# A two-layer decoder on one core: six of eight query tiles by seven block products in place of eight

## The chip, the cores and the metric

The kernel is one program on one core of a Trainium2 chip, written instruction by instruction in a language in which each engine has its own in-order queue and semaphores tie the queues together. The engines are PE (matrix products), DVE (vector), ACT (scalar functions), POOL (general) and SP, which here only starts transfers. POOL starts transfers too. The metric is the time of one execution on the device in microseconds (us).

## The reference

The input is 1024 tokens of width 1024 in float32. Layer 0 mixes tokens with a gated short convolution, layer 1 with sliding-window attention; each is followed by a SwGLU feed-forward network of inner width 2816. What the change touches is the query projection of layer 1:

```python
h = rmsnorm(x, norm_mixer[1])
qkv = h @ w_qkv                      # 1024 x (1024 q + 256 k + 256 v)
q, k = rmsnorm(q, q_gain), rmsnorm(k, k_gain)     # per head of 64
...
scores = einsum('bnqkgd,bnskd->bnkgqs', qb, kw) * scale   # blocks of 128 queries, 256 keys
p = softmax([scores + alibi, masked; sink])[..., :-1]
out = einsum('bnkgqs,bnskd->bnqkgd', p, vw).reshape(1024, 1024) @ w_o
x = x + out
```

There are 16 query heads and 4 key and value heads of 64.

## The kernel before, in words

Activations lie transposed in SBUF, features on partitions and tokens along the free side: `X[k]` is feature block k (128) of the residual stream, 1024 tokens, and `xs[k]` (tags XS0 to XS7) is the normalised operand, kept as a high and a low part in a reduced 32-bit format (`fp32r`). Every large product is a sum of three matmuls of 128x128 weights against 128x512 operands: high by high, high by low, low by high. Weights arrive by SP's transfers in `WR` and are split there into `WH` (high) and `WL` (low) by `Weights.split`, whose cast and subtract go to engines that the caller names.

The convolution, feed-forward and output products already use a scheme of seven block products in place of eight (`SUMS` names which sums of weight blocks it needs; `added_sums` makes these in DRAM by copies on SP and accumulating transfers on POOL). The query projection does not: each of its eight tiles of 128 output features (two heads) is 8 feature blocks times 6 matmuls, 48 in all (`product_step`, lines 161 to 172).

Attention runs so. `project_k` makes the two key tiles `k0` and `k1`, `project_v` two value tiles of 512 tokens. Their results stand in the four PSUM banks of tag "acc" until ACT and DVE have taken them out: `keep_v` scales by the token's factor r, with the high part on ACT and the low on DVE (line 1723); `keep_k` turns the head statistics across partitions with transposes on PE (1746), multiplies the rows by them on DVE (`scale_rows`, 1751), and writes zero-padded high and low halves (1765 to 1767). Query tile 0 follows. Up to here the tile scheduler orders the instructions of each engine. From `keep_q(0, acc)` on, the order is as written: `step` takes one softmax unit (one of 8 query tiles by 8 token blocks) through the letters of

```python
ORDER = "SPTMEDkPHLVOPK"
```

where each P asks the product generator for its next piece, here two matmuls; S is the scores, T and H/L turns, V the product with the values. So a query tile of 24 pieces is 8 steps, and the softmax of unit n runs beside the projection of a later tile, `LAG` steps on.

PSUM has eight banks: four "acc", and P0 to P3. `after_silu` ties instructions to the end of layer 0.

In the layer before, the planner of a `Line` sets the order: `at(t, f)` puts a call at time t of a list by hand, `put` a block product's operands. `half_chain` is a half's token statistics, with `mean`, `guess` and `turn`; `turn` is the transposes that put it across partitions (line 1179 issues them, 1165 makes their input).

## Time and profile before

| | us |
|---|---|
| median of 3 runs | 1933.56 |
| lowest, highest | 1932.24, 1933.91 |
| the profiled execution | 1931.62 |
| its span | 1929.8 |

A profile shows one execution. A row of the timeline has a start, a duration, the engine, the line of the kernel, the operation and its output and input; "x4" means four in a row, and the square bracket names what ended the idle time before. Matmuls overlap, so a matmul's own duration (0.39 us for 128x512) is longer than the distance to the next one's start.

The stretch concerned: layer 0's last product starts at 952.25; the key tiles follow to about 977, the values and the turns to 1005.3, query tile 0 to about 1020, query tiles 1 to 7 to about 1184. Then come the output projection and layer 1's feed-forward network.

### The profile page before, as it was taken

The page shows a single profiled execution, that of the slowest core. Times are in us where ns is not written, and L with a number is a line of the kernel's source. Part 1 is how long each engine was busy: PE and PEld are TensorE (multiplying, and loading weights), DVE is VectorE, ACT ScalarE, POOL GpSimd, SP SyncE. Part 2 cuts the span into 40 slices and gives each one's busy share as a digit, 9 for nine tenths or more (in the row PEclk, how much of TensorE's full clock was granted, in tenths as well). Part 3 has the DMA queues.
Part 4 walks back from the last instruction along what each step waited for, and adds up shares of the span by engine and source line. Part 5 has one row for each costly group of instructions (what it writes and reads, how often), then busy time and mean ns, then how long its engine had stood idle before and what let it go on. Part 6 is the DMA issues. An engine that isn't in the chain of part 4 may idle for free.

```text
span 1929.8 us, 25194 instructions
## 1 busy us (share of the span) xinstructions
PE 1922.1 (100%) x9105; PEld 1608.3 (83%) x9105; DVE 1286.8 (67%) x2223; ACT 877.7 (45%) x1741; POOL 275.7 (14%) x373
## 2 busy tenths in 40 slices
PE   9999999999999999999999999999999999999999
PEld 7888888888888888888898888888888888888887
DVE  8997877975655666555644777788656665665543
ACT  5543464533333334444435887555333333344441
POOL 0011231011101100000014455210111111100000
PEclk9999999999999999999999999999999999999999
DMA  8896695376657638976310000152674576477562
GB/s 314 255 252 144 141 249 156 107 235 191 156 193 210 149 135 298 337 220 206 96 34 23 23 12 18 53 182 76 215 218 135 204 190 166 130 251 267 196 227 102
DMA packets 132077, 326.14 MB, mean 169 GB/s; under 512 B 13680, under 2 KB 25072, under 8 KB 131952
## 3 DMA queue, kind: packets, MB, share of 16 engines
q1 hardware_dynamic: 101520, 228.81, 34.9%
q0 software_dynamic: 30288, 95.70, 20.3%
q8 instruction: 71, 1.16, 0.2%
q14 instruction: 54, 0.44, 0.1%
q10 hardware_dynamic: 144, 0.03, 0.0%
HBM read 261.31 MB, written 130.55 MB: 203 GB/s over the span
## 4 chain that ended last, share of the span: by engine, by line
PE 93%; issue 2%; DVE 2%; DMA 1%; POOL 1%; ACT 1%; SPq 0%; POOLq 0%; ACTq 0%; DVEq 0%
PE acc L996 15%; PE acc L997 15%; PE acc L999 15%; PE P L996 9%; PE P L999 9%; PE P L997 9%; PE acc L167 7%; PE acc L171 3%; PE P L1922 1%; PE P L1746 1%; PE acc L1126 1%; PE P L1947 1%; PE acc L1128 1%; PE acc L1127 1%; PE P L1948 1%
## 5 line engine op out<-in xcount | busy, mean ns | idle before, releaser
L996 PE MATMUL acc<-XS,G 128*128 128x512 f32 x926 | 360.4, 389 | 0.0
L999 PE MATMUL acc<-XS,G 128*128 128x512 f32 x926 | 360.3, 389 | 0.0
L997 PE MATMUL acc<-XS,G 128*128 128x512 f32 x926 | 360.2, 389 | 0.0
L996 PE MATMUL P<-A,G 128*128 128x512 f32 x550 | 214.1, 389 | 0.0
L999 PE MATMUL P<-A,G 128*128 128x512 f32 x550 | 214.0, 389 | 0.0
L997 PE MATMUL P<-A,G 128*128 128x512 f32 x550 | 214.0, 389 | 0.0
L999 PEld LDWEIGHTS acc<-XS,G 128*128 128x128 f32 x926 | 173.9, 188 | 36.1
L996 PEld LDWEIGHTS acc<-XS,G 128*128 128x128 f32 x926 | 173.9, 188 | 36.0
L997 PEld LDWEIGHTS acc<-XS,G 128*128 128x128 f32 x926 | 173.9, 188 | 35.9
L996 PE MATMUL acc<-A,G 128*128 128x512 f32 x442 | 172.1, 389 | 0.0
L999 PE MATMUL acc<-A,G 128*128 128x512 f32 x442 | 172.0, 389 | 0.0
L997 PE MATMUL acc<-A,G 128*128 128x512 f32 x442 | 171.9, 389 | 0.0
L930 DVE TENSOR_TENSOR G<-WR,G 128x512 fp32r<-128x512 f32 (+1 forms) x216 | 144.4, 668 | 29.2 <-ACT G L929 28.4
L930 DVE TENSOR_TENSOR G<-WL,G 128x512 fp32r<-128x512 f32 x168 | 114.9, 685 | 71.1 <-ACT G L929 71.1
L929 ACT CAST G<-WR 128x512 fp32r<-128x512 f32 (+1 forms) x216 | 130.4, 605 | 64.7 <-PE acc L999 27.5
L167 PE MATMUL acc<-XS,WH 128*128 128x512 f32 x480 | 148.2, 408 | 1.1 <-ACT WH L139 0.8
L929 ACT CAST G<-WH 128x512 fp32r<-128x512 f32 (+1 forms) x174 | 104.7, 602 | 86.0 <-PE acc L999 37.8
L930 DVE TENSOR_TENSOR G<-WH,G 128x512 fp32r<-128x512 f32 (+1 forms) x174 | 115.5, 664 | 17.9 <-ACT G L929 17.9
L1327 ACT ACTIVATE G<-G 128x512 f32<-128x512 f32 x88 | 55.8, 634 | 156.8 <-DVE G L1424 151.0
L999 PEld LDWEIGHTS P<-A,G 128*128 128x128 f32 x550 | 103.3, 188 | 21.4
L997 PEld LDWEIGHTS P<-A,G 128*128 128x128 f32 x550 | 103.3, 188 | 21.4
L996 PEld LDWEIGHTS P<-A,G 128*128 128x128 f32 x550 | 103.3, 188 | 21.4
(335 smaller groups left out, 3646.2 us busy)
## 6 DMA issues: line engine op xcount, KB each, us to landing
G<-h SPq DMA_DIRECT2D x70, 512.0 KB, 5.1
s<-in_w_dn SPq DMA_DIRECT2D x32, 704.0 KB, 7.5
h<-X POOLq DMA_DIRECT2D x44, 512.0 KB, 4.6
s<-s POOLq DMA_DIRECT2D x32, 704.0 KB, 7.2
WR<-in_w_gu SPq DMA_DIRECT2D x36, 512.0 KB, 4.6
WH<-in_w_gu SPq DMA_DIRECT2D x36, 512.0 KB, 3.8
h<-X POOLq DMA_DIRECT2D x66, 256.0 KB, 3.3
WR<-s SPq DMA_DIRECT2D x62, 256.0 KB, 3.7
```

Source lines behind the costliest of these rows:

```text
L167: pe.matmul(ps.half(h), wh, xs[:, j, c], start=first and j == 0, stop=False)
L171: pe.matmul(ps.half(h), wl, xs[:, 0, c], start=False, stop=last)
L929: lambda: act.copy(out_hi, raw),
L930: lambda: lo_eng.tensor_tensor(out_lo, raw, plain(out_hi), ALU.subtract),
L996: pe.matmul(ps, w[:, 0, c], x[:, 0, :], start=start and e == 0, stop=False, skip_group_check=True)
L997: pe.matmul(ps, w[:, 0, c], x[:, 1, :], start=False, stop=False, skip_group_check=True)
L999: pe.matmul(ps, w[:, 1, c], x[:, 0, :], start=False, stop=last, skip_group_check=True)
L1126: pe.matmul(ps, hi[:, kc], xs[:, 0, c], start=k == 0, stop=False, skip_group_check=True)
L1127: pe.matmul(ps, hi[:, kc], xs[:, 1, c], start=False, stop=False, skip_group_check=True)
L1128: pe.matmul(ps, lo[:, kc], xs[:, 0, c], start=False, stop=k == n_op - 1, skip_group_check=True)
L1327: state["silu"] = act.activation(x, x, AF.Silu)
L1746: pe.transpose(pb[:, t], wide[:, t], ident)
```

## The change

Query tiles 0 and 1 stay as they were. Tiles 2 to 7 become three pairs; of a pair, the 2x2 blocks (two tiles by the two halves of the tokens, each over even and odd feature blocks) are computed by seven block products of 12 matmuls each, 84 for a pair of tiles in place of 96. `QUERY_ORDER` is the order of the seven. Four of their operands are sums of operand blocks (`operand_sums`: per pair of feature blocks one scale on ACT, four `scalar_tensor_tensor` on DVE, then split in high and low on ACT and DVE); they are stored to `q_ops` in DRAM by POOL, two transfers of 1 MB for each of four calls, and loaded again by SP, 512 KB at a time, for each pair of tiles that uses them (`STREAMED`; 48 loads, in a ring of rooms). The weights come as granules of 256 KB, from a new layout `w_q` of the query weights or from `q_sums`, sums made in layer 0's feed-forward by eight copies and eight accumulating transfers. A granule is split by ACT and POOL.

Other things move. Both key weights are loaded ahead of the value weights. The four `operand_sums` stand between the calls that make keys and values, the last ahead of the second key tile's statistics. `step`'s pieces are two, one, two and two matmuls in turn in the pairs (24 pieces for 42 matmuls). `LAG` is 12. `keep_q` of a paired tile finds its values in SBUF, where DVE and ACT have added the blocks (`finish`), and takes its squares from there. SP is now in the hand-written order too. The output weights' early tiles are split at other steps and under other tags, and the feed-forward of layer 1 names other slots. In layer 0 the second half's `half_chain` and the first `scale` and `put` calls come 1.6 and 1.2 later.

The program has these counts, before and after: PE 128x512 matmuls 7785 and 7749; DVE 16 more `scalar_tensor_tensor` of 128x512, 28 more `tensor_tensor` of 128x512; ACT 18 more casts of 128x256, 16 more casts and 10 more activations of 128x512, 6 fewer copies; POOL 18 more subtracts of 128x256 and 16 more transfers; SP 71 more transfers.

The core of the diff:

```diff
-LAG = 10
+LAG = 12
+QUERY_ORDER = (0, 5, 2, 6, 1, 3, 4)
+STREAMED = (5, 2, 3, 4)
...
-            at(t + 3.9, mean)
-            at(t + 3.95, guess)
-            at(t + 5.7, turn)
+            d = 1.6 if whole and h else 0.0
+            at(t + 3.9 + d, mean)
+            at(t + 3.95 + d, guess)
+            at(t + 5.7 + d, turn)
...
-                at(t + 6.8 + 2.6 * p, scale, 1, 2 * p + 1)
-                put(6, p, lambda p=p: X[2 * p + 1][:, hi_half], t + 7.6 + 2.6 * p, minus=True)
+                at(t + 8.0 + 2.6 * p, scale, 1, 2 * p + 1)
+                put(6, p, lambda p=p: X[2 * p + 1][:, hi_half], t + 8.8 + 2.6 * p, minus=True)
...
+        def operand_sums(p, tags):
+            tiles = [slot(tag, (P, 2, 2, HALF), F32R) for tag in tags]
+            t1, t2, t3, t4 = (a[:, i] for a in tiles for i in (0, 1))
...
+            act.activation(b12, X[even][:, hi_half], AF.Copy, scale=ge)
+            dve.scalar_tensor_tensor(raw(t1), X[even][:, lo_half], ge, b12, ALU.mult, ALU.subtract)
+            dve.scalar_tensor_tensor(raw(t2), X[odd][:, hi_half], mo, raw(t1), ALU.mult, ALU.subtract)
+            dve.scalar_tensor_tensor(raw(t3), X[odd][:, hi_half], go, b12, ALU.mult, ALU.subtract)
+            dve.scalar_tensor_tensor(raw(t4), X[odd][:, lo_half], mo, raw(t2), ALU.mult, ALU.subtract)
+            for t in (t1, t2, t3, t4):
+                act.copy(t[:, 0], raw(t))
+                dve.tensor_tensor(t[:, 1], raw(t), plain(t[:, 0]), ALU.subtract)
+            for i, a in enumerate(tiles):
+                nc.gpsimd.dma_start(
+                    q_ops[p, 2 * i : 2 * i + 2].rearrange("k p c -> p k c"), plain(a).rearrange("p k j c -> p k (j c)")
+                )
...
+        for g in range(2):
+            w_k.append(Weights())
+            w_k[g].load(w_qk[NK + g], 0, NK)
         k0 = project_k(0)
+        operand_sums(0, ("A2", "A3"))
...
+        operand_sums(1, ("A0", "A1"))
         r = token_r()
...
+        operand_sums(2, ("A4", "A5"))
+        v += [slot(f"A{4 + q}", (P, 4, NKV, 2, HD), F32R) for q in range(2)]
         v_ps = project_v(0)
         keep_v(0, v_ps)
         keep_k(0, k0[0], y0)
+        operand_sums(3, ("A2", "A3"))
         st = bank("acc")
         head_stats(st, k1[1], 0, NB)
...
+            def split_granule(j, i):
+                g, c = grans[j % 2], slice(i * 2 * P, (i + 1) * 2 * P)
+                act.copy(g[:, 0, c], raws[:, j % 2, c])
+                pool.tensor_tensor(g[:, 1, c], raws[:, j % 2, c], plain(g[:, 0, c]), ALU.subtract)
...
+                for j, (u, k) in enumerate(seq):
+                    plan(0, lambda j=j: split_granule(j + 1, 0))
+                    plan(0.5, lambda j=j: split_granule(j + 1, 1))
+                    load_granule(j + 2)
...
+                    for p in range(NK // 2):
+                        x = operand(k, p)
...
+                        for i, (w, b) in enumerate(((0, 0), (0, 1), (1, 0))):
+                            pe.matmul(
+                                ps, g[:, w, c], x[:, b, :], start=begin and i == 0, stop=end and i == 2, skip_group_check=True
+                            )
+                            n += 1
...
+                            if last and k in STREAMED:
+                                after_use(used["n"])
+                                used["n"] += 1
+                            if last and end:
+                                finish(u, k)
+                            if n % 7 in (2, 4, 5, 0):
+                                yield
...
-        with tc.manual_schedule(engines={E.PE, E.Activation, E.DVE, E.Pool}):
+        with tc.manual_schedule(engines={E.PE, E.Activation, E.DVE, E.Pool, E.SP}):
             keep_q(0, acc)
             w = load_w(w_qk[1], NK, dve, pool)
+            pairs = query_pairs()
...
+            keep_q(1, acc, pairs.odd_raw)
+            work = pairs.work()
+            for _ in range(NB * (NK - 2)):
...
+                step(work)
+            run(work)
```

In the program the engines' queues change at these places. First DVE, at the end of the values and the second key tile. Names: `A_1123` and `A_1163` are value tiles, `acc` the banks that hold the projected values, `G_1151` (before) and `G_1154` (after) the second key tile, `G_1131` the first. Before:

```order
L1723 SCALAR_TENSOR_TENSOR A_1123_7690<-acc_8033,r_7774,A_1123_7690 128x4x64
L1723 SCALAR_TENSOR_TENSOR A_1123_7690<-acc_8082,r_7774,A_1123_7690 128x4x64
L1751 TENSOR_TENSOR G_1151_7860<-G_1151_7860,P_1171_8141 128x512
L1723 SCALAR_TENSOR_TENSOR A_1123_7690<-acc_8082,r_7774,A_1123_7690 128x4x64
L1751 TENSOR_TENSOR G_1151_7860<-G_1151_7860,P_1172_8148 128x512
L1765 CAST A_1173_8154<-G_1151_7860 64x1024 x2
L1766 TENSOR_TENSOR A_1174_8155<-G_1151_7860,A_1173_8154 64x1024
L1767 TENSOR_TENSOR A_1174_8155<-G_1151_7860,A_1173_8154 64x1024
L1766 TENSOR_TENSOR A_1174_8155<-G_1151_7860,A_1173_8154 64x1024
L1767 TENSOR_TENSOR A_1174_8155<-G_1151_7860,A_1173_8154 64x1024
```

The value subtracts (L1723) stand among the row scalings of the second key tile (L1751), ahead of its split (L1765 to L1767). The changed program, from just behind the two row scalings of the second key tile (L1786):

```order
L1724 SCALAR_TENSOR_TENSOR A_1171_8086<-X_885_6220,cst_61,A_1172_8087 128x512
L1726 SCALAR_TENSOR_TENSOR A_1172_8087<-X_890_6243,cst_61,A_1172_8087 128x512
L1725 SCALAR_TENSOR_TENSOR A_1171_8086<-X_890_6243,minus_gain_7707,A_1171_8086 128x512
L1730 TENSOR_TENSOR A_1172_8087<-A_1172_8087 128x512
L1800 CAST A_1169_8076<-G_1131_7776 64x1024 x2
L1727 SCALAR_TENSOR_TENSOR A_1172_8087<-X_890_6243,minus_gain_7707,A_1171_8086 128x512
L1730 TENSOR_TENSOR A_1171_8086<-A_1171_8086 128x512 x2
L1801 TENSOR_TENSOR A_1170_8077<-G_1131_7776,A_1169_8076 64x1024
L1802 TENSOR_TENSOR A_1170_8077<-G_1131_7776,A_1169_8076 64x1024
L1801 TENSOR_TENSOR A_1170_8077<-G_1131_7776,A_1169_8076 64x1024
L1802 TENSOR_TENSOR A_1170_8077<-G_1131_7776,A_1169_8076 64x1024
L1757 SCALAR_TENSOR_TENSOR A_1162_7953<-acc_7955,r_7828,A_1162_7953 128x4x64
```

Three sums of the last `operand_sums` call (L1724 to L1726), a fourth (L1727), its subtracts (L1730) and the first key tile's split (L1800 to L1802) now stand between the row scaling and the first value subtract (L1757); seven more value subtracts follow, with the last L1730 after the second of them, and then the second key tile's split.

On POOL, at the same place, before:

```order
L1775 MEMSET G_1124_7691 128x64
L142 ISA
L142 TENSOR_TENSOR WL_8167<-WR_8164,WH_8166 128x1024
L893 DMA s_1_113<-s_1_113 256x512
L142 TENSOR_TENSOR WL_8225<-WR_8222,WH_8224 128x1024
L142 TENSOR_TENSOR WL_8239<-WR_8228,WH_8238 128x256 x2
```

The changed program, where `A_1160` to `A_1172` are the sums of the last two calls, and `WL_8255` and `WL_8313` the low weights of query tiles 0 and 1:

```order
L1732 DMA q_ops<-A_1160_7936 128x2x1024
L1732 DMA q_ops<-A_1161_7937 128x2x1024
L1732 DMA q_ops<-A_1171_8086 128x2x1024
L1732 DMA q_ops<-A_1172_8087 128x2x1024
L145 ISA
L145 TENSOR_TENSOR WL_8255<-WR_8252,WH_8254 128x1024
L145 TENSOR_TENSOR WL_8313<-WR_8310,WH_8312 128x1024
```

The low weights of tile 0, which before stood behind the memset and the configuration alone, now stand behind the eight stores.

On PE, inside a softmax step, with `acc` the projected query, L1879 and L1880 the scores, L1922 and L1746 turns, L1947 and L1948 the product with the values. Before:

```order
L167 MATMUL acc_8558<-XS_1117_7588,WH_8349 128x512
L167 MATMUL acc_8559<-XS_1117_7588,WH_8349 128x512
L1922 MATMUL P_1281_8833<-cst_61,G_1124_7691 128x128 x4
L167 MATMUL acc_8558<-XS_1117_7588,WH_8349 128x512
L167 MATMUL acc_8559<-XS_1117_7588,WH_8349 128x512
L1947 MATMUL P_1283_8848<-G_1278_8813,A_1122_7689 128x256
L1948 MATMUL P_1283_8848<-G_1278_8813,A_1122_7689 128x256
L1947 MATMUL P_1283_8848<-G_1278_8813,A_1122_7689 128x256
L1948 MATMUL P_1283_8848<-G_1278_8813,A_1122_7689 128x256
L171 MATMUL acc_8558<-XS_1117_7588,WL_8350 128x512
L171 MATMUL acc_8559<-XS_1117_7588,WL_8350 128x512
```

Changed (L1913 and L1914 are the scores, L1956 and L1781 turns, L1981 and L1982 the values, L2269 the pairs' products):

```order
L2269 MATMUL acc_8908<-WH_8318,WL_8321 128x512 x2
L1913 MATMUL P_1319_9164<-A_1169_8076,G_1288_8966 128x192
L1914 MATMUL P_1319_9164<-A_1170_8077,G_1288_8966 128x192
L1913 MATMUL P_1319_9164<-A_1169_8076,G_1288_8966 128x192
L1914 MATMUL P_1319_9164<-A_1170_8077,G_1288_8966 128x192
L2269 MATMUL acc_8908<-WH_8318,WL_8321 128x512
L1956 MATMUL P_1320_9171<-cst_61,G_1123_7709 128x128 x2
L1781 MATMUL P_1321_9178<-cst_61,s_1307_9088 128x128 x4
L2269 MATMUL acc_8908<-XS_1100_7490,WL_8321 128x512 x2
L1981 MATMUL P_1323_9192<-G_1316_9145,A_1163_7954 128x256
L1982 MATMUL P_1323_9192<-G_1316_9145,A_1163_7954 128x256
L1981 MATMUL P_1323_9192<-G_1316_9145,A_1163_7954 128x256
```

Pieces of two matmuls at each place have become pieces of two, one and two; the fourth, of two, stands behind the last row shown.

## Prediction

> **What bounds the kernel now.** I read the page first: the engines' shares, then the chain that ended last, then what PE waited for over the whole span.

> ```profile
> PE 1922.1 (100%) x9105; PEld 1608.3 (83%) x9105; DVE 1286.8 (67%) x2223; ACT 877.7 (45%) x1741; POOL 275.7 (14%) x373
> PE 93%; issue 2%; DVE 2%; DMA 1%; POOL 1%; ACT 1%; SPq 0%; POOLq 0%; ACTq 0%; DVEq 0%
> PE P L323 <- DVE s L320: 1.5, 1, 1.5
> PE P L1179 <- DVE s L1165: 1.2, 1, 1.2
> PE acc L167 <- ACT WH L139: 0.8, 1, 0.8
> PE acc L167 <- DVE A L1723: 0.2, 1, 0.2
> ```

> PE is busy all the time, 93% of the chain is PE, and its waits on other engines come to 3.7 us, in four places. So a matmul less is worth its pitch, wherever it is, as long as PE's feeders hold; and a new wait of PE is paid in full, since there is no slack to swallow it. The sum therefore has two sides: matmuls removed, and waits taken away or made.

> The profiled execution took 1931.62 us, 1.94 below the median of the runs, 1933.56. I sum against the first and add 1.9 at the end.

> **Matmuls removed.** In the program order PE has 36 matmuls of 128x512 fewer. Their pitch, from the key projection, where the same six-matmul steps run:

> ```profile
> 956.58 1.09 PE L167 MATMUL acc<-XS,WH 128*128 128x512 f32 x4
> ...
> 964.76 1.07 PE L167 MATMUL acc<-XS,WH 128*128 128x512 f32 x4
> ```

> Between these two starts lie six steps, 36 matmuls: 8.18 us, 227 ns each. The change takes away 36: **-8.2 us**. (Three pairs of tiles at 7/8 of 96 would save 36; that is the whole of it. The tile that stays, 0, and tile 1 are untouched.)

> **Two small waits.**

> ```profile
> 325.16 0.39 PE L999 MATMUL acc<-XS,XS 128*128 128x512 f32 x1
> 326.72 1.02 PE L1179 MATMUL P<-cst,s 128*128 128x1 f32 x8 [1.18 <-DVE s L1165]
> 953.98 1.04 ACT L139 CAST WH<-WR 128x1024 fp32r<-128x1024 f32 x1 [6.82 <-DMA WR<-in_w_qk]
> 954.45 1.22 DVE L142 TENSOR_TENSOR WL<-WR,WH 128x1024 fp32r<-128x1024 f32 x1
> 955.08 1.20 PE L167 MATMUL acc<-XS,WH 128*128 128x512 f32 x4 [0.75 <-ACT WH L139]
> 956.12 0.62 PE L171 MATMUL acc<-XS,WL 128*128 128x512 f32 x2
> ```

> Layer 0's statistic transposes stand in PE's queue where DVE isn't ready, and PE idles 1.2 us. The half's statistics (mean, guess, turn) are put 1.6 us later in the planned order, more than the wait, so PE does about seven other matmuls there: **-1.2** (bounds -1.2 and 0, if the four `scale` calls put 1.2 us later make the next operands late; each takes one STT of 0.66, below, every 2.6 us, so there is room).

> At the first key product PE waits 0.75 for ACT's split of weights that have just landed: SP loaded them behind the value weights. Now they come first, and that wait goes. But the low half is still made on DVE, which is in the operand sums and layer 0's last additions there. If its subtract starts no earlier than the 954.45 of now, it ends at 955.7, and the first low product starts then in place of 956.12: **-0.4** (bounds: -0.8, all of the wait, and +1.2, one more such subtract ahead of it).

> **The large term: query tile 0 starts late.** The four `operand_sums` put 16 STT, 16 subtracts, and 20 ACT operations into the stretch from 952 to 1020, which DVE has time for in the sum, but each has a place in a queue. The last is called just before the statistics of the second key tile, and in the program order DVE has its rows behind the row scaling of that second tile (line 1786 after, 1751 before); then come `keep_k`'s halves of the first tile, and only then `keep_v`'s subtracts of both value tiles (1757 after, 1723 before). Those subtracts free the four "acc" banks of PSUM, which the query tiles 0 and 1 need. Before, they stood ahead of the long rows:

> ```profile
> 1004.53 1.03 PE L1746 MATMUL P<-cst,G 128*128 128x128 f32 x8
> 1005.32 1.41 PE L167 MATMUL acc<-XS,WH 128*128 128x512 f32 x5
> 1006.89 0.94 PE L167 MATMUL acc<-XS,WH 128*128 128x512 f32 x3 [0.17 <-DVE A L1723]
> 1007.67 0.62 PE L171 MATMUL acc<-XS,WL 128*128 128x512 f32 x2
> 1005.63 0.68 DVE L1751 TENSOR_TENSOR G<-G,P 128x512 f32<-128x512 f32 x1
> 1006.26 0.48 DVE L1723 SCALAR_TENSOR_TENSOR A<-acc,r,A 128x256 fp32r<-128x256 f32 x1
> 1007.38 1.39 DVE L1765 CAST A<-G 64x1024 fp32r<-64x1024 f32 x2
> 1008.78 1.22 DVE L1766 TENSOR_TENSOR A<-G,A 64x1024 fp32r<-64x1024 f32 x1
> 940.14 2.65 DVE XS L1503 x4
> ```

> The reader sees the last key turn end near 1005.1 (its second half starts it), the banks freed one by one while DVE does L1751 and L1723 alternately, a wait of PE of only 0.17, and the first low product at 1007.67. The long `keep_k` subtracts (1.22 each) of the second tile came behind all that, those of the first long before it. DVE's in-order row in the changed program, begun at 1005.1 with the same turns: two row scalings 2 x 0.63 (start to start), three STT 3 x 0.66 (the chain's 2.65 for four), a subtract of the scalings' shape 0.63, the two casts 1.39, one STT 0.66, two subtracts 1.26, four long subtracts 4 x 1.23 = 4.92, then `keep_v` 2 x 0.40 (from 1006.26 to 1006.66) and the last split 0.63. These add to 13.5, so DVE ends the last split at 1018.6. Two more `keep_v` rows free tile 0's banks, by 1019.4, and four more tile 1's, by 1021.0; tile 1's first four products stand ahead of tile 0's first low one in PE's order.

> Next, POOL. Tile 0's low weights are one POOL subtract, and it stands behind the last of the eight stores to `q_ops`, which waits for that last split. Before, nothing stood ahead of it:

> ```profile
> 954.82 0.14 POOL L1775 MEMSET G<- 128x64 f32 x1
> 966.79 2.40 POOL L142 TENSOR_TENSOR WL<-WR,WH 128x1024 fp32r<-128x1024 f32 x1 [11.83 <-DVE WH L141]
> L142 POOLq MODIFY_POOL_CONFIG  x2: 2/2/2, 954.9 to 954.9; - x2
> L925 POOL DMA_DIRECT2D s<-A x4: 754/766/901, 33.0 to 56.2; - x4
> DMA to landing us min/median/max: 4.7/6.7/6.9
> ```

> A store of the same size takes POOL 0.77 to issue, so 1018.6 + 0.8 = 1019.4; the subtract takes 2.40: 1021.8; the first low product starts at 1022.0 in place of 1007.67: **+14.3 us**. PE can do only the high products of tiles 0 and 1 in the meantime, and the low ones then follow without a gap; no work stands behind it that PE could take instead, as PE is in order and the scores need tile 0. What is queued behind the waiting subtract on POOL (tile 1's low weights, the spreads) moves with it. By the banks alone it is 1021.0 and four products, the same 1022. The bounds: +12 if each DVE row is a sixth shorter, and +17 if DVE's row also waits on ACT for the scale or a half of the sums.

> **Clock.** PE then has idled for most of 13 us.

> ```profile
> 1925.00:1930.00 5.00, 0.85 (x4) 0.38 (x2) 0.69 (x1) 0.00 (x0) 0.00 (x0) 0.80 0.14 52
> L323 PE MATMUL P<-s 128*128 128x512 f32 x9 | 4.2, 650 | 1.5 <-DVE s L320 1.5
> ```

> At the end of the kernel, after PE stops, the granted clock (the sixth figure behind the stretch, 0.80) drops within 5 us. The nine matmuls with which the kernel starts take 4.2 us, where nine of 227 ns take 2.05: a cold start costs 2.1. Some of the slow stretch falls on the high products, which run while PE waits anyway; I take **+1.2** (bounds 0 and 2.1). [...]

> **The pairs.** A tile costs 42 matmuls in place of 48, in the same number of softmax steps, so the softmax work per us of PE grows. ACT is nearest to its limit there:

> ```profile
> 1140.00:1160.00 20.00, 20.00 (x140) 17.98 (x138) 16.37 (x48) 18.01 (x55) 12.30 (x16) 1.00 0.05 15
> sum 140.00, PE 139.99 PEld 125.07 DVE 103.69 ACT 116.59 POOL 69.40; mean PE 20.00 PEld 17.87 DVE 14.81 ACT 16.66 POOL 9.91
> 1093.14 0.41 ACT L139 CAST WH<-WR 128x256 fp32r<-128x256 f32 x1
> 1093.45 0.46 ACT L1914 ACTIVATE G<-G,mx 128x192 f32<-128x192 f32 x1
> G<-h SPq DMA_DIRECT2D x70, 512.0 KB, 5.1
> GB/s 314 255 252 144 141 249 156 107 235 191 156 193 210 149 135 298 337 220 206 96 34 23 23 12 18 53 182 76 215 218 135 204 190 166 130 251 267 196 227 102
> ```

> The sum row is for 1040 to 1180 in stretches of 20: ACT 116.6 of 140, 83%. Three casts more a tile, 18 at 0.31 (the two starts), are 5.6, and the stretch gets 8.2 shorter: 122.2 of 131.8, 93%; in the fullest stretch ACT is at 90% now. DVE gets 12 additions, four a pair, at 0.63: 103.7 + 7.6 of 131.8, from 74% to 84%. The lag of 12 steps in place of 10 buys slack. Bounds 0 and +6 (18 casts on the path); I take **+0.5**. Streamed operands: 48 loads of 512 KB. The nearest row, 512 KB by SP, lands in 5.1; the ring holds five operands, each used for three matmuls (0.7 us) among others, and a room is reloaded as its use ends, about 4 uses of a streamed product and up to three other products ahead. 25.2 MB and 21 loads of weights of 256 KB, 5.5 MB, in some 135 us are 227 GB/s; attention moved 12 to 34 a slice, and other slices of the page up to 337. Cost 0, covered by the ring; if that cover is gone, a late operand costs PE the difference, up to 5 each.

> Nothing else is on the path: the block sums of `w_q` are 8 copies and 8 adding transfers more in layer 0's feed-forward, off the chain; the output projection begins two steps later in the softmax's count, with its own products as cover.

> **Sum.** -8.2 - 1.2 - 0.4 + 14.3 + 1.2 + 0.5 = **+6.2**: 1937.7 for a profiled execution, **1939.6** on the median's footing. The range runs from the smaller wait of rival 4 to the reload of rival 1 with 1 us of ACT beside it: 1934.5 to 1946.5.

> **Rivals.**
> 1. [...] Chance 0.18.
> 2. *The sums don't delay `keep_v`, and the kernel is faster.* If the wait and the clock together cost less than 9.3 us, the gains outweigh them; with a wait of 5 (DVE gets through the sums before 1005 because X and ACT's scale are ready early, or the tags free sooner) it ends near 1929. Against it: DVE is in order, and the sums stand behind row scalings that need turns at 1004.5. By that order the wait is at least 7 (the four long subtracts and two STT). Chance 0.09.
> 3. *Attention becomes bound by ACT or by late operands.* ACT at 93% with waits that don't fit together, or rooms reloaded late: +5 beside the forecast, 1944.5. For it: 18.01 of 20 in one stretch; against: only one such stretch. Chance 0.12.
> 4. *The wait is there but smaller*, 8 to 11 us, because what isn't in DVE's way goes earlier: within 0.2% of now, 1934.5. Chance 0.13.

> My forecast itself has 0.48. 0.2% (3.9 us) is about what a measurement of this kernel can tell from no change. Faster takes rival 2 (0.09); same takes rival 4 and the low edge of the forecast, 0.19; slower the rest, 0.72.

> **What would show it.** In the profile after: PE's longest wait is that of tile 0's products between about 1005 and 1022, put down to DVE's line 1757 and to POOL's line 145; DVE's row from 1005 on reads scaling, three STT, subtracts, long subtracts, then 1757; the granted clock is under 1.00 there; L1179's wait is gone; from tile 2 on PE has no wait, and query tiles 2 to 7 take 8.2 less. [...] The forecast is wrong if DVE takes 1757 before the sums, or if any wait above 2 us appears from tile 2 on.

## The result, and the profile after

The changed kernel takes 1965.30 us (median of 5 runs, 1962.81 to 1966.82), the kernel before, run beside it, 1933.91: 1.0162 of it, 95% interval 1.0147 to 1.0177, 31.4 us slower. The forecast was 1939.6 and a range of 1934.5 to 1946.5. The profiled execution took 1966.82 us, its span is 1965.0.

The page's first lines on the engines and the chain, and then PE's waits on other engines of 0.8 us and more (us in total, times, longest):

```profile
PE 1929.9 (98%) x9069; PEld 1608.9 (82%) x9069; DVE 1313.8 (67%) x2268; ACT 894.2 (46%) x1779; POOL 301.4 (15%) x407
PE 90%; DVE 4%; ACT 3%; issue 1%; DMA 1%; POOL 0%; DVEq 0%; POOLq 0%; ACTq 0%; SPq 0%
PE acc L170 <- DVE A L1757: 13.8, 1, 13.8
PE P L1981 <- DVE G L2000: 5.4, 2, 2.7
PE P L1668 <- DVE A L2028: 1.8, 1, 1.8
PE acc L1131 <- ACT A L934: 1.8, 1, 1.8
PE P L326 <- DVE s L323: 1.5, 1, 1.5
PE acc L174 <- DVE WL L145: 1.4, 2, 1.0
PE acc L2269 <- POOL WL L2211: 1.3, 1, 1.3
PE P L1913 <- DVE mx L1928: 0.9, 2, 0.6
PE P L1781 <- DVE A L2028: 0.9, 1, 0.9
PE acc L1133 <- DVE WH L935: 0.8, 1, 0.8
```

PE was 100% busy and 93% of the chain; now ACT and DVE have 7% of the chain between them. The first wait is the one forecast, and L326's 1.5 stood at the start of the kernel before too (L323 there). The others were not forecast: most lie in the pairs (L1981, L2269, L1913), in the output projection (L1668, L1781) and at the start of the last feed-forward network (L1131, L1133); L174's lie in the key tiles. PE's wait on L1179 in layer 0 is gone, as said.

How much each stretch costs comes from the starts of PE's matmuls: the distance of each to the next, less the median distance of the same two shapes in the kernel before, added up. "Long" are excesses over 0.5 us, "short" those of 0.04 to 0.5, in which a slow clock counts too.

| stretch of the changed kernel | long, us | short, us | before, same work: long, short |
|---|---|---|---|
| query tiles 0, 1 (1004.6 to 1040) | 14.0 | 2.6 | 0, 1.1 |
| pairs (1040 to 1200) | 9.3 | 13.9 | 0, 5.1 |
| output projection (1200 to 1281) | 4.0 | 3.8 | 0, 2.1 |
| start of the last network (1281 to 1331) | 1.9 | 1.7 | 0, 0.4 |

Together 51.2 against 8.7, 42.5 more; less the 8.2 of the removed matmuls that is 34.3 of the 35.2 by which the spans differ.

The late start, as it happened: PE's last turns and its wait, DVE's row, and POOL behind it.

```profile
1004.68 1.04 PE L1781 MATMUL P<-cst,G 128*128 128x128 f32 x8
1019.48 3.95 PE L170 MATMUL acc<-XS,WH 128*128 128x512 f32 x8 [13.76 <-DVE A L1757]
1023.23 1.05 PE L174 MATMUL acc<-XS,WL 128*128 128x512 f32 x2
1006.52 0.74 DVE L1724 SCALAR_TENSOR_TENSOR A<-X,cst,A 128x512 f32<-128x512 f32 x1
1016.30 1.22 DVE L1802 TENSOR_TENSOR A<-G,A 64x1024 fp32r<-64x1024 f32 x1
1017.55 0.88 DVE L1757 SCALAR_TENSOR_TENSOR A<-acc,r,A 128x256 fp32r<-128x256 f32 x2
1018.35 0.68 DVE L1730 TENSOR_TENSOR A<-A 128x512 fp32r<-128x512 f32 x1
1019.66 0.71 POOL L1732 DMA_DIRECT2D q_ops<-A  x1 [5.86 <-ACT A L1756]
1020.48 4.71 POOL L145 TENSOR_TENSOR WL<-WR,WH 128x1024 fp32r<-128x1024 f32 x2
```

DVE goes through the sums and the first key tile's split and reaches the first value subtract (L1757) at 1017.55; the last split ends at 1019.03 (forecast 1018.6). POOL stores at 1019.66 and starts the two low subtracts 0.11 after that store ends, some 2.4 each. PE does nothing until the banks are free at 1019.48; then come eight high products, 0.47 apart at half the clock (0.50 granted from 1010.76 to 1024.41), and the first low product starts at 1023.23; the forecast said 1022.0. POOL's first low subtract has ended by then, so the banks, and not the stores, held PE.

What the forecast did not have, at the start of the second pair: two rows of ACT, with 3 us between them, the POOL row that ends that time, and PE's last product before its wait and the first behind it.

```profile
1094.64 0.18 ACT L1948 ACTIVATION_READ_ACCUMULATOR G<-G,mx 128x1 f32 x1
1097.82 0.59 ACT L2228 COPY G<-acc 128x512 f32<-128x512 f32 x1 [2.99 <-POOL G L1870]
1096.52 1.27 POOL L1870 TENSOR_TENSOR G<-G,G 64x512 fp32r<-64x512 f32 x1
1096.97 0.47 PE L2269 MATMUL acc<-XS,WL 128*128 128x512 f32 x1
1100.13 0.58 PE L1981 MATMUL P<-G,A 128*128 128x256 f32 x1 [2.69 <-DVE G L2000]
  POOL G L1870: 6.9, 3
```

L2228 takes a pair's first block out of PSUM into the buffer G7, which `keep_q` of the previous pair's even tile still reads: its last low part (L1870) is on POOL, which is late. ACT is in order, so the casts and exponents behind the copy wait, DVE behind them, and PE's values (L1981) last. The last row is from the view of line 2228: 6.9 us of ACT's idle time in its three executions. PE stands for 2.7 in two of them.

### The profile page after: what moved, and what is told of

It is laid out like the page before. It is cut to its first block, busy times and chain, and to the rows that moved or that the text cites. A ratio compares the mean times of both kernels' runs of the same rounds, so it can differ in the third digit from the quotient of the medians.

```text
span 1965.0 us, 25426 instructions
## 1 busy us (share of the span) xinstructions
PE 1929.9 (98%) x9069; PEld 1608.9 (82%) x9069; DVE 1313.8 (67%) x2268; ACT 894.2 (46%) x1779; POOL 301.4 (15%) x407
## 4 chain that ended last, share of the span: by engine, by line
PE 90%; DVE 4%; ACT 3%; issue 1%; DMA 1%; POOL 0%; DVEq 0%; POOLq 0%; ACTq 0%; SPq 0%
PE acc L1001 16%; PE acc L1004 16%; PE acc L1002 16%; PE P L1001 9%; PE P L1002 9%; PE P L1004 9%; PE acc L170 3%; PE acc L174 2%; PE acc L2269 2%; PE P L1956 1%; PE P L1781 1%; PE P L1981 1%; DMA WR<-in_w_o 1%; PE P L1982 1%; PE P L1913 0%
## 5 line engine op out<-in xcount | busy, mean ns | idle before, releaser
L934 ACT CAST G<-WL 128x512 fp32r<-128x512 f32 x168 | 103.3, 615 | 30.8 <-DVE WL L883 17.3
## 6 DMA issues: line engine op xcount, KB each, us to landing
G<-h SPq DMA_DIRECT2D x70, 512.0 KB, 4.9
h<-X POOLq DMA_DIRECT2D x44, 512.0 KB, 4.5
WR<-in_w_gu SPq DMA_DIRECT2D x36, 512.0 KB, 5.0
WH<-in_w_gu SPq DMA_DIRECT2D x36, 512.0 KB, 4.3
XS<-q_ops SPq DMA_DIRECT2D x36, 512.0 KB, 4.8
```

The source lines that it names most:

```text
L934: lambda: act.copy(out_hi, raw),
```

## The experiments

Two theories at first. A: the loss is two stalls of their own place, the late start and ACT's copy, each with the slow clock behind it. B: the streamed pairs are bound by ACT or by transfers, and the stalls only show it.

**Stores on SP** (e1). In `operand_sums`:

```diff
-                nc.gpsimd.dma_start(
+                nc.sync.dma_start(
                     q_ops[p, 2 * i : 2 * i + 2]...
```

> The changed kernel, with the eight stores of the operand sums started by SP in place of POOL. In the program order DVE then has the four calls' sums ahead of the values' subtracts, and tile 0's low weights stand behind no store. Theory A (the time went to two places of its own: query tile 0's late start, 14.0 us of idle PE and about 1.5 of slow clock behind it, and the pairs' own stalls): PE's wait of 13.8 goes, the rest stays, so about 15.5 less than the changed kernel: 1950. Theory B (the streamed pairs have ACT or the transfers as their bound, and the late start only fills slack): the pairs end hardly sooner, 1960 or more.

1949.91, 15.4 less than the changed kernel. The wait of 13.8 is 0.2; the others stay, in this run's waits of PE:

```profile
PE P L1981 <- DVE G L2000: 5.4, 2, 2.7
PE P L1668 <- DVE A L2028: 1.8, 1, 1.8
PE acc L170 <- DVE A L1757: 0.2, 1, 0.2
```

So the late start cost about what was forecast for it (14.3 + 1.2); some 1 us of the 15.4 is another wait that went with it, L174's in the key tiles (1.4 before this edit, 0.3 with it). The order that made it came from the issuing engine: with POOL as the issuer, the scheduler put the last call's sums behind the second key tile and the values' subtracts behind them; with SP all four calls' sums come before (DVE's last row of them ends at 980.8 in e1's trace).

**The copy a step later** (e2), and **both** (e3):

```diff
-                    soon(lambda: act.copy(even[:, lo_half], ps))
+                    plan(1, lambda: act.copy(even[:, lo_half], ps))
```

> The changed kernel, with one ACT copy moved: the first block of a pair goes out of its PSUM bank one softmax step later than now. It writes the buffer that still holds the previous pair's even tile, which POOL reads last. Theory A (ACT, in order, waits 3 us for POOL at this copy, PE runs out of work behind it, and the granted clock falls for 6 us after): the two gaps of 3.2 us at the pairs' starts go, and the two stretches of half clock with them, 2 x (2.9 + 2.3): 10 us less than the changed kernel, 1955. Theory B (ACT or POOL is full there, and the wait only shows it): the gaps move to other waits and the time stays within 3 us of 1965.

> Both of the two edits: stores by SP, and the pairs' first copy a step later. Theory A: both savings add, 25.5 less than the changed kernel: 1940. What is left above the kernel before is then the stalls behind the pairs (tail of attention, 8 us with their clock) less the 8 us of the removed products. Theory B: less than 20 in all, since one stall takes the other's place.

E2: 1958.92, 6.4 less, where 10 was expected. E3: 1943.53, 6.4 less than e1: the two add exactly, but together they take 21.8 in place of 25.5. The two gaps of 3.2 us are gone; PE now loses time in the pairs in small pieces. So A holds for both stalls, and something of B is left.

**The small parts on the kernel before** (e4): the lines of the diff on `half_chain`, `scale`, `put` and `w_k`, no others.

> The kernel before, with only the two small parts of the change: key weights loaded first, and layer 0's second half-statistics and scales later. As forecast: 1.6 us less than before (1.2 and 0.4). By the trace after, which shows layer 0 ending 0.7 sooner and the key tiles losing 0.9 of it again: no change, within 0.5 of before.

1930.35 against 1933.53, ratio 0.9984 (0.9974 to 0.9993): 3.2 us less, 1.3 to 5.0 by the interval. That takes in the forecast's 1.6 and rules out that nothing changed. PE's waits on L1165 and on L139 are both gone. In the changed kernel the key tiles lose part of it again, since DVE's low weights (L145, 1.0) then wait behind the sums.

For the rest of B there were now theory C, that ACT's load makes the small waits, and theory D, that they come from the chain's length and the lag.

**The granules' high parts on POOL** (e5, on e3):

```diff
-                act.copy(g[:, 0, c], raws[:, j % 2, c])
+                pool.tensor_copy(g[:, 0, c], raws[:, j % 2, c])
```

> As the run with both edits (1943.5), and the high part of each weight granule is cast on POOL in place of ACT, which takes some 0.6 us of ACT per granule, a tenth of its work in the pairs. Theory C (ACT, busy for 16 to 18 of 20 us in the pairs, is what makes PE's many small waits there): PE's time beyond its pitches between 1050 and 1160 falls by more than half, 4 to 6 us less: 1938 to 1940. Theory D (the waits come from the chain through DVE and the step's own length, and from the lag): within 2 us of 1943.5, or slower where POOL's later low parts make PE wait.

1935.07, 8.5 less than e3: C, and by more than it said. The size is loose: e5's seven times spread from 1933.6 to 1939.8, and three of them, the profiled one (1938.81) among them, are only some 4 below e3. E3's waits from 1060 to 1150, the same DVE wait in the kernel before and in e5, and a new wait of e5's PE show the path:

```profile
POOL WL L2211 <- ACT WL L2210: 29.8, 17, 6.0
DVE G L1969 <- ACT G L1963: 15.6, 15, 1.6
DVE G L1935 <- ACT G L1929: 9.8, 13, 1.1
DVE G L1969 <- ACT G L1963: 10.2, 13, 1.3
PE acc L2269 <- POOL WL L2210: 1.8, 1, 1.8
```

DVE's subtract in the softmax waits for ACT's cast of the turned scores, 15.6 us in place of 9.8 (third row, before); with e5 it is 10.2. PE's next product stands behind that subtract. Few of PE's own waits there are long enough to be listed (0.7 us in e3), so the last step rests on the order of the rows and on how the three figures move. The fifth row is what the edit costs: PE waits 1.8 for the first granule, in place of 1.3.

**A lag of 11** (e6, on e3): `LAG = 11`, and `later=2` for the odd tiles.

> As the run with both edits, with the softmax 11 steps behind the projection in place of 12, and the odd tile's statistics 2 steps later in place of 3. Theory D (part of the loss is that the softmax ends two steps nearer to the end of the output projection, so that what follows is late): a third to half of the 4.9 us that PE loses between 1240 and 1310 goes, 2 us less: 1941.5. Theory C: no change from the lag, 1943.5, or more where a query tile's parts are now late for its scores.

1939.20, 4.3 less. Between 1240 and 1309 PE loses 2.7 in place of 4.5, as D expected; but in the pairs there are new waits (L1913 and L1781 on POOL's L1870, 2.6 us in all): the query parts are now late. D holds for the tail. The rest of the 4.3 has no one place.

**The first two granules' low parts on DVE** (e7, on e3):

```diff
-                pool.tensor_tensor(g[:, 1, c], ...)
+                (dve if j < 2 else pool).tensor_tensor(g[:, 1, c], ...)
```

> As the run with both edits, with the low parts of the first two weight granules on DVE in place of POOL. PE waits 1.3 us there for POOL, which is behind three 1.3 us subtracts of query tile 0, and the granted clock is at half for 3.3 us behind it. If that is the cause, the wait and the slow stretch go: 1.4 + 1.65 = 3 us less, 1940.5. If the next granule or an operand is as late, 1943.

1940.27, 3.3 less, as expected; PE's wait on L2211 is gone.

**The kernel before with a lag of 12** (e8): that line and nothing else.

> The kernel before, with the softmax 12 steps behind the projection in place of 10 and nothing else. Theory D: the softmax ends two steps later, and the end of the attention layer and the start of the last feed-forward network lose time by that alone: 2 to 5 us slower, 1936 to 1938. Theory C: the lag costs nothing without the pairs: within 0.2% of before.

1965.68, 32.7 more: neither theory. The lag did far more than end the softmax later. At each of five tile borders, here the second:

```profile
1085.13 0.60 ACT L1802 ACTIVATE G<-acc 128x512 f32<-128x512 f32 x1 [3.08 <-PE P L1880]
1086.21 0.98 PE L1922 MATMUL P<-cst,G 128*128 128x128 f32 x4 [0.63 <-ACT G L1914]
1088.33 1.86 PE L1658 MATMUL P<-cst,G 128*128 128x2 f32 x8 [1.14 <-DVE G L1935]
1088.00:1096.00 8.00, 7.67 (x33) 7.15 (x34) 4.07 (x16) 4.07 (x15) 1.20 (x2) 0.57 0.00 1
PE acc L1126 <- ACT A L929: 1.8, 1, 1.8
PE acc L1128 <- DVE WH L930: 0.8, 1, 0.8
```

ACT's square (L1802) writes G5 or G6, the buffer from which PE still takes scores (L1880) of the older tile; ACT stands 3.08, PE behind it twice, and the granted clock is 0.57 over the next 8 us (fourth row). It is the kind of stall that the pairs have at L2228, by another buffer. So e8 does not show what the lag costs in the changed kernel, whose tiles are kept at other steps. Its last two rows do: the waits at the start of the last network are those of the changed kernel to a tenth (1.8 and 0.8), and have no pairs behind them.

**All that took something** (e9): e3, e5 from the third granule on, e7, and the last odd tile's statistics half a step later, so that PE has products between L1781 and L1668, which use one PSUM bank:

```diff
-                    keep_q(2 * u + 1, None, *raw_of_odd(u), later=3)
+                    keep_q(2 * u + 1, None, *raw_of_odd(u), later=3 if u < 3 else 3.5)
```

**And the end of the projection** (e10, e11): `plan(0.5 + i, f)` for the casts of the last two output tiles becomes `plan(1.5 + i, f)` and `plan(2.5 + i, f)`.

> The edits that took something, together (stores by SP, the pairs' first copy a step later, granule highs on POOL from the third on, the first two granules' lows on DVE), and one more: the last odd tile's statistics half a step later, so that PE has products between two uses of one PSUM bank there. Theory C (ACT's load and the in-order waits on shared buffers and banks are the whole loss in the pairs): 1935 less 2.0 at the first granules, 3.6 at the bank (2.0 and its slow clock), 1.1 behind it: 1928.5. If the saved waits come back elsewhere in the pairs: 1932 or more.

> As the run with all these edits, and at the end of the output projection ACT's casts of two late output tiles, which wait for the last softmax, stand one step later, behind the first of two weight casts for the feed-forward network. If these casts keep ACT and with it the network's first weights waiting (PE waits 0.8 and 1.8 there), half of these 3.2 us goes: 1.5 less than that run.

> The same with the casts two steps later, behind both weight casts: both waits go, 3 us less than the run without (1925.5). If the late tiles themselves are then what the network waits for, no less than the run with one step.

E9: 1927.87, near the 1928.5 of theory C. Against e5 it is 7.2 less: 3.3 is what e7 took, and 3.9 is left for the bank, whose two waits (L1668, L1781) are gone. No run has the edit at the bank alone, and the 3.9 inherits e5's spread. E10: 1925.30, 2.6 less again, more than the half expected: both waits are gone with one step. E11: 1926.17, no better. PE's waits in e9 and, below the "...", all that e10 has:

```profile
PE acc L1131 <- ACT A L934: 1.0, 1, 1.0
PE acc L1133 <- DVE WH L935: 0.9, 1, 0.9
...
PE P L326 <- DVE s L323: 1.5, 1, 1.5
PE acc L174 <- DVE WL L145: 0.3, 1, 0.3
PE P L1001 <- DVE G L1372: 0.3, 1, 0.3
PE acc L170 <- DVE A L1757: 0.2, 1, 0.2
```

E10 is faster than both kernels: 0.9965 of the kernel before, 0.9953 to 0.9978. The gains that the forecast summed, without its wait, clock and ACT terms, come to 1923.8.

**ACT's load by itself** (e12): e10, with `act` in place of `pool` for the high part of every granule from the third on.

> As the fastest run (1925.3), with the high part of every weight granule back on ACT, where the change had it; nothing else differs. Theory C (ACT's load alone makes PE wait in the pairs, 8 us in the run in which only this was changed): the waits come back, 5 to 8 us slower, 1930 to 1933. Theory E (it was ACT's load together with the wait on the shared bank and the first granules that cost, and without those ACT has slack): within 2 us, 1926.

1932.91, 7.6 more than e10: theory C, with all the larger stalls out of the way. (The kernel before, run beside e12, was 0.9 above the one beside e10, so 6.7 may be nearer.) DVE's wait for ACT's cast from 1040 to 1170, and the sums over 1040 to 1200 in stretches of 20, each for e12 and then e10:

```profile
DVE G L1969 <- ACT G L1963: 21.3, 19, 1.6
...
DVE G L1969 <- ACT G L1963: 16.1, 20, 1.3
...
sum 160.00, PE 158.09 PEld 137.82 DVE 123.83 ACT 132.75 POOL 88.08; mean PE 19.76 PEld 17.23 DVE 15.48 ACT 16.59 POOL 11.01
...
sum 160.00, PE 159.77 PEld 142.28 DVE 129.51 ACT 128.52 POOL 106.68; mean PE 19.97 PEld 17.79 DVE 16.19 ACT 16.06 POOL 13.34
```

ACT is busy 83% in the first and 80% in the second, where more of the program passes in the same time. Neither is near a full engine. Not all of the 7.6 is waiting: in e12's profile the clock is twice at half in the pairs, for 3.4 us each, and never in e10's, so half of these 6.8, some 3.4 us, is by this estimate the slow clock's share.

## Why the prediction was wrong

- *Query tile 0's late start, +14.3, and its clock, +1.2*: right in place and price, and in DVE's order; e1 took 15.4. Two details were not: PE did no high products meanwhile but stood from 1005.72 to 1019.48, and the eight of them then ran at half the clock on the path; and POOL's stores did not hold PE.
- *Matmuls removed, -8.2*: the traces have the 36 fewer (9105 and 9069). Their price is not tested alone: e10 is 7.3 below the kernel before, with these and the small waits in it, 9.8 by the forecast.
- *Small waits, -1.6*: right in sign; 3.2 in e4, with an interval that takes in 1.6.
- *The top of the range, 1946.5, with rival 1's reload*: no run shows a reload on POOL; in the changed kernel the low subtract starts 0.11 us after the last store ends.
- *Streamed operands, 0*: right; PE has no wait on a transfer in the pairs, and e10, which streams the same operands, has no wait of PE there at all.
- *Two sums*: 1931.62 + 6.2 is 1937.8, 0.1 above the figure given, and rival 2's "at least 7" comes to 6.2 from its own rows (4 x 1.23 and 2 x 0.66). Neither matters to the result.
- **The step that failed is "The pairs", +0.5, with bounds of 0 and +6, and "Nothing else is on the path".** Without the late start the forecast was 1924.1 and e1 1949.9, 25.8 more. The runs place it: 6.4 at the copy into a buffer still read (e3), 8.5 in the small waits behind ACT and the slow clock that goes with them (e5; 7.6 in e12), 3.3 at the first granules (e7), 3.9 at the shared bank (e9 less e7's part), 2.6 at the start of the last network (e10): 24.7. These steps follow one another from e1 to e10, so their sum is the distance between those two by construction and checks nothing. The table above checks their places from one trace: it has 18.1 more than before in the pairs (the runs 18.2 for copy, ACT and granules), 5.7 in the output projection (3.9) and 3.2 at the last network (2.6). The prediction's own sign of being wrong, a wait above 2 us from tile 2 on, is there twice (2.7 at L1981).

The working took ACT's share of busy time, 93% by its estimate, as the measure of what ACT can cost. ACT was not that full (83% over the pairs in e12). What cost was order: an in-order ACT behind one copy, and PE's next product behind a cast that came a few tenths later than before. Of this the prediction had the words ("ACT at 93% with waits that don't fit together", rival 3, +5 at a chance of 0.12) and a fifth of the price. It had walked the order of DVE and POOL row by row at query tile 0, and had found that wait to within 1.2 us; it did not walk ACT's row past the first pair's border, where the copy and POOL's last reader of its buffer stand, nor the steps of the tail that the lag moves by two, which it took for covered. That a lag of 12 "buys slack" no run bears out: 11 was 4.3 us faster in e6.

## What to carry to other kernels

Where the bound engine has no slack, follow every in-order queue through one whole period of the changed loop, and ask of each write which reader of that buffer is still to come on which engine; a share of busy time tells nothing of that. A sum of small waits with a slow clock behind them can be as dear as one long stall (here 8.5 us in e5, and 6.4 in e3 for the two stalls at the copy). Moving the lag between two pipelined loops changes which buffers meet, so it is costed as a change of its own. The engine that starts a transfer can decide the order of other engines, where a scheduler sets it.

## What the runs showed of the hardware that was not expected

The granted clock falls to 0.50 behind stalls that look harmless. Stretches of the changed kernel (the sixth figure behind the stretch is the clock): around the pair's stall, around the wait at the bank, and at the start of the last network; the last row is of e12.

```profile
1100.00:1106.00 6.00, 5.87 (x22) 5.28 (x23) 3.11 (x12) 5.49 (x16) 4.26 (x5) 0.50 0.27 98
1214.00:1220.00 6.00, 6.00 (x30) 5.36 (x31) 1.91 (x7) 2.60 (x10) 0.35 (x1) 0.72 0.01 3
1296.00:1302.00 6.00, 4.23 (x17) 2.43 (x15) 4.40 (x8) 3.33 (x6) 0.54 (x1) 1.00 0.53 169
1088.00:1090.00 2.00, 2.00 (x11) 1.82 (x10) 1.84 (x9) 0.87 (x4) 0.61 (x2) 0.50 0.82 262
```

After PE's wait of 2.7 it is at half for 6 us, with PE busy for 5.87 of them: some 3 us lost, an estimate (half of the 6), as much again as the stall. After 1.8 (the bank) it falls at 1215.56, with PE back at work since 1213.91; after 1.8 at the last network it does not (1.00). In e12 it is at half at 1088, with a single wait of PE, of 0.2, listed from 1070 to 1092. At the end of the kernel before, whose row of 0.80 the prediction shows, the last matmul ends at 1925.85 and the clock falls at 1928.03, 2.2 us later.

```profile
1084.18 1.95 PE L1668 MATMUL P<-cst,G 128*128 128x2 f32 x16
```

Whether these products, with two columns each, have a part in the fall was not tested. What makes the clock fall stays open.
